# Page numbers bounded once on chip, and one register load for both parts of a value unit, in a decoder step on one core

## The chip, the cores and the metric

The kernel runs on one core of a Trainium2 chip. The metric is the device time of one execution in microseconds (us). The kernel before takes 4163.96 us, the median of 3 runs (4162.37 to 4166.68).

## The reference, cut to what matters

Two layers of a decoder are computed for a prompt (1024 tokens) and, with the same weights, for 8 sample sequences of 4 new tokens each. Everything is in float32. The change touches one part alone, how the samples read their past: 4096 old tokens for each of the 8, which lie in a pool of 320 pages of 128 tokens, at places that a table names.

```python
for l in range(DEPTH):                       # 2 layers
    xp, kp, vp, sp, cp, fp = trunk_layer(xp, lp, l, p_pos, ..., None, None, mk_p, mv_p, ...)   # the prompt
    past_k = cache_k[l][page_table].reshape(Bs, past_len, 2 * DIFF_H, DIFF_DH)   # page_table: 8 x 32 page numbers
    past_v = cache_v[l][page_table].reshape(Bs, past_len, DIFF_H, DIFF_DV)
    xs, ks_, vs_, ss, cs, fs = trunk_layer(xs, lp, l, s_pos, ..., past_k, past_v, ...)          # the samples

# trunk_layer, on h = rms_norm(x)
z = h @ w_in                                 # gated DeltaNet heads and differential attention heads side by side
x = x + concat([o_gdn, o_diff]) @ w_out
x = x + memory_attention(...) @ w_co         # cross-attention into 256 memory tokens
gt = causal_dwconv(hf @ w_gate)              # gated MLP, 2816 wide
x = x + (silu(gt) * (hf @ w_up)) @ w_down
```

## The kernel before, in words

**The prompt stream.** Per layer it projects (`w_in`), runs the DeltaNet heads and the causal attention, then the output projection, the cross-attention and the MLP. A float32 product is three matmuls of split operands. A weight unit is fetched into a `raw` tile by `fetch` (L359, a DMA issued by SyncE, here SP), ScalarE (ACT) copies it to `whi` (L376), GpSimd (POOL) makes `wlo` (L377), and TensorE (PE) multiplies. From the output projection on there are two `raw` slots, so a fetch may start when `wlo` of the unit before the last one is made. Just ahead of the output projection, `ot` tiles (two slots) bring the heads' outputs and eight DMAs bring back the residual (`x<-xsc`, L1826). In attention, `akT` and `aq` are the keys and queries, read back from DRAM (`qksc`).

**The sample stream.** `dec()` runs beside the prompt stream. A unit is 4 pages of one sequence, of keys or of values, 64 units of each kind in a layer. A unit is loaded in two halves, and each half fills one of four ring slots. A key half (`kn`) is 2 pages, whole: 2 DMAs of 256 KB. A value half (`vn`) is two quarters of each of the 4 pages: 4 DMAs of 128 KB, so the two value halves name the same 4 pages. Keys are transposed on VectorE (DVE, tile `T`) and multiplied into `psB`; values are multiplied into `psC`.

**How a page is addressed.** `pages` (L715) reads the page numbers from the row `pt_sb` in SBUF into SP's registers with one TENSOR_LOAD for each half, and with `min_val` and `max_val` given, each register is then checked: a FUSED_REGOPS computes whether it lies within the pool, and a SEQ_ASSERT reads that. After that each DMA has its own FUSED_REGOPS for its address, then a MOVE, then the issue itself (L724). All of this runs in order on SP, which also issues the weight fetches and most other DMAs.

**Order.** The program is written as generators that are interleaved by weights. Then a scheduler sets each engine's order with a timeline of its own, in which an instruction's cost plays a part. `issue_after` holds an instruction behind another: the page load stands behind the last page DMA and behind the last weight fetch written before it (`anchor`).

Of the kernel before, what the change touches and what calls it, by code (L numbers as in the profile page):

```python
# [9 lines left out]
F32 = mybir.dt.float32  # L10
# [4 lines left out]
ALU = mybir.AluOpType  # L15
# [8 lines left out]
NB = 8  # L24
# [6 lines left out]
NPG = PAST // P  # L31
# [154 lines left out]
def build(tc, a, out, depth=2):  # L186
    nc = tc.nc
# [38 lines left out]
    v_, s_, g_, t_ = Tracked(nc.vector), nc.scalar, nc.gpsimd, Tracked(nc.tensor)  # L226
# [273 lines left out]
    lp = lp_cm.__enter__()  # L500
# [30 lines left out]
    for t in range(9):  # L531
        n = P if t < 8 else NS
# [13 lines left out]
    for k0 in range(0, KT, 3):  # L546
# [3 lines left out]
        for k in range(m):  # L550
            if (k0 + k) % 2 == 0:
                t = dk.tile([P, 1056], F32R, name="pre", tag="pg", bufs=PGB).rearrange("p (a b c) -> p a b c", a=2, b=2)
# [8 lines left out]
        nc.sync.dma_start(xsc[:, :, csl(c)], x[:, :, csl(c)])  # L561
    pt_sb = cp.tile([1, NB * NPG], I32, name="pt_sb")
    nc.sync.dma_start(pt_sb, a["page_table"].rearrange("b n -> (b n)").unsqueeze(0))

    def scalars():
        for l in range(1, depth):
            params(l, nc.sync)
        for l in range(depth):
            lam_init = 0.8 - 0.6 * math.exp(-0.3 * l)
            lq = lp.tile([P, 4, 64], F32, name="lq", tag="lq", bufs=1)  # L570
            for k, nm in enumerate(("lam_q1", "lam_q2", "lam_k1", "lam_k2")):
                nc.sync.dma_start(lq[:, k, :], pbc(a[nm][l:l + 1, :]))
            pr = lp.tile([P, 2, 64], F32, name="pr", tag="pr")
            v_.tensor_tensor(pr, lq[:, 0:2], lq[:, 2:4], op=ALU.mult)
            sm = lp.tile([P, 2], F32, name="sm", tag="sm")
            v_.tensor_reduce(sm, pr, axis=AX.X, op=ALU.add)
            ex = lp.tile([P, 2], F32, name="ex", tag="ex")
            s_.activation(ex, sm, AF.Exp)
            nl = cp.tile([P, 1], F32, name=f"nlam{l}")
            v_.tensor_tensor(nl, ex[:, 1:2], ex[:, 0:1], op=ALU.subtract)  # L580
            v_.tensor_scalar(nl, nl, -lam_init, None, op0=ALU.add)
            lam_t.append(nl)
            ab = cp.tile([P, 2, 4], F32, name=f"ab{l}")
            nc.sync.dma_start(ab[:, 0, :], pbc(a["a_log"][l:l + 1, :]))
            nc.sync.dma_start(ab[:, 1, :], pbc(a["dt_bias"][l:l + 1, :]))
            abs_ = cp.tile([P, 2], F32, name=f"abs{l}")
            for h in range(4):
                v_.tensor_copy(abs_[32 * h:32 * h + 32, :], ab[32 * h:32 * h + 32, :, h])
            gate_b.append((ab, abs_))
# [76 lines left out]
    for l in range(depth):  # L666
# [23 lines left out]
        ckl, cvl = a["cache_k"][l], a["cache_v"][l]  # L690
        npool = ckl.shape[0]
# [13 lines left out]
        def ring(sh, nm, dt=F32):  # L705
            return dtile(sh, nm, "pg", PGB, 1056, dt)
# [6 lines left out]
                st_.enter_context(tc.issue_after(anchor[-1].ins))  # L713
                last_page.append(nc.sync.dma_start(dst, src))

        def pages(pg, n, dst, src):

            with ExitStack() as st_:
                if last_page:
                    st_.enter_context(tc.issue_after(last_page[-1].ins))  # L720
                st_.enter_context(tc.issue_after(anchor[-1].ins))
                _, regs = nc.values_load_multi_w_load_instructions(pt_sb[0:1, pg:pg + n], engines=(mybir.EngineType.SP,), min_val=0, max_val=npool - 1)
            for i, r in enumerate(regs):
                dma = nc.sync.dma_start(dst(i), src(r))  # L724
            last_page.append(dma)
# [7 lines left out]
        def dec():  # L733
# [15 lines left out]
            def load(i):  # L749
                if i >= 2 * len(seq):  # L750
                    return
                kind, b, S = seq[i // 2]
                hf = i % 2
                t = halves[i] = ring([P, 2, 512], kind + "n")
                if kind == "k":
                    pages(b * NPG + S * 4 + 2 * hf, 2, lambda j: t[:, j, :], lambda r: ckl[bass.ds(r, 1)].rearrange("o t h d -> (o t) (h d)"))
                else:
                    pages(b * NPG + S * 4, 4, lambda j: t[32 * j:32 * j + 32, :, :], lambda r: cvl[bass.ds(r, 1)].rearrange("o (i b) h e -> (o b) i (h e)", i=4)[:, 2 * hf:2 * hf + 2, :])

            cur = {}  # L760

# [41 lines left out]
            for i in range(PGB - 1):  # L803
                load(i)
            yield 0.1
            pT = po = None
            for i, (kind, b, S) in enumerate(seq):
                if kind == "k":
                    T = dtile([P, 4, 16, 32], "T", "T")
                    if b == 1 and S == 0:  # L810
                        queries(1)
                    for hf in range(2):
                        load(2 * i + hf + PGB - 1)
                        t = halves.pop(2 * i + hf)
                        with behind(v_):
                            v_.transpose(T[:, 2 * hf:2 * hf + 2].rearrange("p s j b -> p (s j b)"), t.rearrange("p s d -> p (s d)"))
                        yield 0.45
                    products(b, S, T)
                    yield 0.3
                    if b and S == 2:  # L820
                        pT = yield from transposed(b - 1)
                    continue
# [4 lines left out]
                if S == 1 and b + 2 < NB:  # L827
                    queries(b + 2)
                load(2 * i + PGB - 1)
                yield 0.5  # L830
                load(2 * i + PGB)
# [1530 lines left out]
        if more:  # L2362

            ws = []
            with prio(TPRI):
                for k0 in range(0, KT, 3):
# [3 lines left out]
                    for k in range(m):  # L2370
                        if (k0 + k) % 2 == 0:
                            t = ring([P, 2, 2, 264], "pre", F32R)
# [30 lines left out]
def program(inputs, depth=2):  # L2403
    import concourse.bacc as bacc

    nc = bacc.Bacc("TRN2", target_bir_lowering=False, num_devices=1)
    arrays, aps, outs = {}, {}, {}
    for name in _INS:
        arr = np.ascontiguousarray(inputs[name])
        arrays[f"in_{name}_dram"] = arr  # L2410
        aps[name] = nc.dram_tensor(f"in_{name}_dram", arr.shape, mybir.dt.from_np(arr.dtype), kind="ExternalInput").ap()
    arrays["in_cst_dram"] = CONST
    aps["cst"] = nc.dram_tensor("in_cst_dram", CONST.shape, F32, kind="ExternalInput").ap()
    for name, shape in _OUTS:
        outs[name] = nc.dram_tensor(f"out_{name}_dram", shape, F32, kind="ExternalOutput").ap()
    with tile.TileContext(nc, schedule_with_timeline_sim=True) as tc:
        build(tc, aps, outs, depth)
    return nc, arrays
# [8 lines left out]
```

## Time and profile before

| | |
|---|---|
| median of 3 runs | 4163.96 us |
| the profiled execution | 4172.92 us |
| its span, first to last instruction | 4171.1 us |
| TensorE busy | 3863.1 us (93%) |
| VectorE, ScalarE, GpSimd busy | 2256.6, 1311.7, 1174.7 us |
| mean granted TensorE clock | 0.957 of 2.4 GHz |
| page DMAs (keys, values) | 512 of 256 KB, 1024 of 128 KB |

SP has no line in the table of busy engines, because issuing a DMA and register work count as the sequencer's. Its instructions are found by their source line: L722 is the register load and its checks, L724 the page DMAs, L359 the weight fetches. "SPq" in a row is SP's sequencer. The profiled execution is 8.96 us longer than the median, so a sum over the trace is subtracted from 4172.92 and then set against the median.

### The profile page before, as it was taken

The numbers are of one execution on the slowest core, as the hardware profiler recorded it, in microseconds if no ns is written. First come the engines' busy times: TensorE is split into PE (matmuls) and PEld (weight loads), VectorE is DVE, ScalarE is ACT, GpSimd is POOL, SyncE is SP. The second block draws the span as 40 slices with busy tenths as digits, with TensorE's granted clock in tenths as the row PEclk, the third lists the DMA queues.
The fourth block names the chain that finished last, engine by engine and source line by source line (L and its number), as shares of the span: only waits on it lengthen the run. The fifth ranks groups of instructions, "written<-read, shape, count | busy, mean of one in ns | idle before, by whom it ended". The sixth has DMA issues, their size and how long they took to land. (4 is left out here: it accounts for less than half of the span.)

```text
span 4171.1 us, 72714 instructions
## 1 busy us (share of the span) xinstructions
PE 3863.1 (93%) x25178; PEld 2988.1 (72%) x25178; DVE 2256.6 (54%) x3907; ACT 1311.7 (31%) x2823; POOL 1174.7 (28%) x1125
## 2 busy tenths in 40 slices
PE   6899979979899999999979998889799999999999
PEld 5789866756667766776769987567566766677667
DVE  7355556863676544343367466577465734443334
ACT  4333424441442212321243253333334312222111
POOL 6452412222322212112246242132231311212211
PEclk8999979999999999999989999799899999999999
DMA  5464587647545543447427565764754455444751
GB/s 176 130 192 147 164 225 192 188 131 214 153 127 163 176 145 110 144 152 227 135 83 219 154 173 182 203 199 130 224 170 125 141 168 154 122 132 133 222 169 61
DMA packets 626469, 673.14 MB, mean 161 GB/s; under 512 B 76875, under 2 KB 444438, under 8 KB 626102
## 3 DMA queue, kind: packets, MB, share of 16 engines
q1 hardware_dynamic: 581475, 638.35, 51.4%
q10 hardware_dynamic: 42963, 25.81, 2.0%
q8 instruction: 200, 3.28, 0.3%
q0 software_dynamic: 1664, 4.33, 0.3%
q14 instruction: 167, 1.37, 0.1%
HBM read 588.12 MB, written 80.17 MB: 160 GB/s over the span
## 5 line engine op out<-in xcount | busy, mean ns | idle before, releaser
L377 POOL TENSOR_TENSOR wlo<-raw,whi 128x1024 fp32r<-128x1024 f32 (+1 forms) x308 | 531.0, 1736 | 1454.5 <-ACT whi L376 1349.5
L219 PE MATMUL psA<-hh,whi 128*128 128x512 f32 (+1 forms) x2096 | 794.1, 379 | 52.5 <-ACT whi L376 22.0
L219 PE MATMUL psA<-hl,whi 128*128 128x512 f32 (+1 forms) x2096 | 790.2, 377 | 4.4 <-DVE hl L219 2.7
L219 PE MATMUL psA<-hh,wlo 128*128 128x512 f32 (+1 forms) x2096 | 788.2, 376 | 0.0
L219 PEld LDWEIGHTS psA<-hh,whi 128*128 128x128 f32 x2096 | 399.7, 191 | 167.2 <-issue 34.0
L376 ACT CAST whi<-raw 128x1024 fp32r<-128x1024 f32 (+1 forms) x308 | 237.7, 781 | 766.0 <-PE psA L219 405.4
L219 PEld LDWEIGHTS psA<-hh,wlo 128*128 128x128 f32 x2096 | 399.2, 190 | 84.9 <-issue 27.2
L219 PEld LDWEIGHTS psA<-hl,whi 128*128 128x128 f32 x2096 | 400.9, 191 | 77.6 <-issue 14.9
L219 DVE STREAM_TRANSPOSE T<-kn 128x1024 f32<-128x1024 f32 x256 | 308.8, 1227 | 119.3 <-PE psB L219 109.6
L219 DVE TENSOR_TENSOR x<-x,psA 128x512 f32<-128x512 f32 x296 | 201.0, 683 | 248.0 <-PE psA L219 239.0
L219 DVE TENSOR_SCALAR fcv<-fraw,pvf 128x1024 f32<-128x1024 f32 x44 | 94.3, 2142 | 352.4 <-ACT fraw L2037 330.1
L219 PE MATMUL psG<-hh,whi 128*128 128x512 f32 x560 | 227.2, 406 | 0.9 <-ACT whi L376 0.9
L219 PE MATMUL psG<-hl,whi 128*128 128x512 f32 x560 | 225.6, 403 | 1.0 <-DVE hl L219 1.0
L219 PE MATMUL psG<-hh,wlo 128*128 128x512 f32 x560 | 223.8, 400 | 0.0
L219 PE MATMUL psA<-hi,hh 128*128 128x256 f32 (+1 forms) x720 | 205.4, 286 | 5.2 <-DVE cxn L219 4.1
L219 PE MATMUL psA<-ah,whi 128*128 128x512 f32 x484 | 195.7, 406 | 10.7 <-ACT whi L376 10.7
L219 PE MATMUL psA<-lo,hh 128*128 128x256 f32 (+1 forms) x720 | 203.8, 283 | 0.6 <-POOL lo L391 0.6
L219 PE MATMUL psA<-hi,hl 128*128 128x256 f32 (+1 forms) x720 | 204.4, 284 | 0.0
L219 PE MATMUL psA<-al,whi 128*128 128x512 f32 x484 | 195.0, 404 | 0.0
L219 PE MATMUL psA<-ah,wlo 128*128 128x512 f32 x484 | 193.9, 402 | 0.0
L219 PE MATMUL psA<-akT,aq 128*128 128x512 f32 (+7 forms) x384 | 154.5, 452 | 30.6 <-DMA aq<-qksc 30.6
L219 PE MATMUL psC<-vn,pT 128*32 128x512 f32 x1024 | 171.6, 626 | 7.8 <-DMA vn<-in_cache_v_dram 7.8
(516 smaller groups left out, 7331.0 us busy)
## 6 DMA issues: line engine op xcount, KB each, us to landing
kn<-in_cache_k_dram SPq DMA_DIRECT2D x512, 256.0 KB
vn<-in_cache_v_dram SPq DMA_DIRECT2D x1024, 128.0 KB
raw<-in_w_gate_dram SPq DMA_DIRECT2D x44, 512.0 KB
raw<-in_w_up_dram SPq DMA_DIRECT2D x44, 512.0 KB
raw<-in_w_down_dram SPq DMA_DIRECT2D x44, 512.0 KB
sw<-in_w_down_dram SPq DMA_DIRECT2D x44, 512.0 KB
sw<-in_w_gate_dram SPq DMA_DIRECT2D x48, 384.0 KB
sw<-in_w_up_dram SPq DMA_DIRECT2D x48, 384.0 KB
```

The lines of the kernel that those rows point to most:

```text
L219: r = f(*args, **kw)
L376: s_.copy(hi, raw)
L377: g_.tensor_tensor(lo, raw, hi.bitcast(F32), op=ALU.subtract)
```

## The change

Three instructions on VectorE now bound the row of page numbers once: to float, clamped to 0 and 319, back to integers. The numbers fit a float exactly, and the table's values lie within the pool, so nothing changes in them. With that, the check at each load is dropped (`skip_runtime_bounds_check_because`). And `pages` takes a key: the first half of a value unit keeps its 4 registers in `kept`, and the second half takes them from there instead of loading them again. Since only the load stood under `issue_after`, the second half's DMAs no longer stand behind the last weight fetch.

```diff
     pt_sb = cp.tile([1, NB * NPG], I32, name="pt_sb")
     nc.sync.dma_start(pt_sb, a["page_table"].rearrange("b n -> (b n)").unsqueeze(0))
+    ptf = lp.tile([1, NB * NPG], F32, name="ptf")
+    v_.tensor_copy(ptf, pt_sb)
+    v_.tensor_scalar(ptf, ptf, 0.0, float(a["cache_k"].shape[1] - 1), op0=ALU.max, op1=ALU.min)
+    v_.tensor_copy(pt_sb, ptf)
...
-        def pages(pg, n, dst, src):
+        kept = {}
+
+        def pages(pg, n, dst, src, keep=None):
 
             with ExitStack() as st_:
                 if last_page:
                     st_.enter_context(tc.issue_after(last_page[-1].ins))
                 st_.enter_context(tc.issue_after(anchor[-1].ins))
-                _, regs = nc.values_load_multi_w_load_instructions(pt_sb[0:1, pg:pg + n], engines=(mybir.EngineType.SP,), min_val=0, max_val=npool - 1)
+                regs = kept.pop(keep, None)
+                if regs is None:
+                    _, regs = nc.values_load_multi_w_load_instructions(pt_sb[0:1, pg:pg + n], engines=(mybir.EngineType.SP,), min_val=0, max_val=npool - 1, skip_runtime_bounds_check_because="the numbers were bounded on chip to those of the pool")
+                    if keep is not None:
+                        kept[keep] = regs
             for i, r in enumerate(regs):
                 dma = nc.sync.dma_start(dst(i), src(r))
             last_page.append(dma)
...
-                    pages(b * NPG + S * 4, 4, lambda j: t[32 * j:32 * j + 32, :, :], lambda r: cvl[bass.ds(r, 1)].rearrange("o (i b) h e -> (o b) i (h e)", i=4)[:, 2 * hf:2 * hf + 2, :])
+                    pages(b * NPG + S * 4, 4, lambda j: t[32 * j:32 * j + 32, :, :], lambda r: cvl[bass.ds(r, 1)].rearrange("o (i b) h e -> (o b) i (h e)", i=4)[:, 2 * hf:2 * hf + 2, :], (b, S))
```

The scheduler costs the shorter program anew, so the order moves. The next rows are SP's, before, in the MLP of layer 0, up to the eighth fetch of `w_down`. ISA is a register instruction, "ISA x8" are the four checks of a value half (a FUSED_REGOPS and a SEQ_ASSERT each), a single ISA is a DMA's address.

```order
L724 DMA vn_21739<-in_cache_v_dram 32x2x512
L722 TENSOR_LOAD pt_sb_425
L722 ISA x8
L724 ISA
L724 DMA vn_21810<-in_cache_v_dram 32x2x512
L724 ISA
L724 DMA vn_21810<-in_cache_v_dram 32x2x512
L724 ISA
L724 DMA vn_21810<-in_cache_v_dram 32x2x512
L724 ISA
L724 DMA vn_21810<-in_cache_v_dram 32x2x512
L359 DMA raw_21864<-in_w_down_dram 128x1024
```

The rows up to the same fetch now:

```order
L734 DMA vn_16041<-in_cache_v_dram 32x2x512
L734 ISA
L734 DMA vn_16041<-in_cache_v_dram 32x2x512
L734 ISA
L734 DMA vn_16084<-in_cache_v_dram 32x2x512
L734 ISA
L734 DMA vn_16084<-in_cache_v_dram 32x2x512
L734 ISA
L734 DMA vn_16084<-in_cache_v_dram 32x2x512
L734 ISA
L734 DMA vn_16084<-in_cache_v_dram 32x2x512
L359 DMA raw_16371<-in_w_down_dram 128x1024
```

The checks are gone, and between the two halves of a unit (`vn_16041`, `vn_16084`) no load stands any more. The fetch itself has moved: before it stood behind 456 value DMAs of the layer, now behind 416, so ten halves were ahead of it that now come after it. Of the 132 fetches of `w_gate`, `w_up` and `w_down` in the prompt stream, 26 moved against the page DMAs, 25 of them ahead and one behind. TensorE's order at this place is the same in both programs.

At the end of layer 0's projection SP's rows before are these, up to a fetch of `w_in` (the 80th of its kind):

```order
L722 TENSOR_LOAD pt_sb_425
L722 ISA x4
L724 ISA
L724 DMA kn_7521<-in_cache_k_dram 128x512
L724 ISA
L724 DMA kn_7521<-in_cache_k_dram 128x512
L722 TENSOR_LOAD pt_sb_425
L722 ISA x4
L359 DMA raw_7839<-in_w_in_dram 128x2x128
```

And now:

```order
L730 TENSOR_LOAD pt_sb_425
L734 ISA
L734 DMA kn_6228<-in_cache_k_dram 128x512
L734 ISA
L734 DMA kn_6228<-in_cache_k_dram 128x512
L997 DMA gdsc_80<-cdst_6312 128x1056
L1011 DMA out_p_gdn_conv_dram<-cso_6456 3x128
L1012 DMA out_s_gdn_conv_dram<-cso_6456 24x128
L359 DMA raw_6735<-in_w_in_dram 128x2x128
```

Eight key DMAs (four halves) that stood ahead of this fetch now come after it. On VectorE, in the prologue, the three new instructions stand among those of the first norms:

```order
L219 CAST ptf_427<-pt_sb_425 1x256
L219 TENSOR_TENSOR pr_792<-lq_787 128x128
L219 TENSOR_SCALAR ptf_427<-ptf_427 1x256
L219 TENSOR_REDUCE sm_794<-pr_792 128x2
L219 CAST pt_sb_425<-ptf_427 1x256
L219 TENSOR_TENSOR hl1_119<-nhf_224,hh1_117 128x2x352
```

## Rows read from the trace of the kernel before

**Rows 1.** The page: busy time, share of the span, instructions of each engine.
```profile
PE 3863.1 (93%) x25178; PEld 2988.1 (72%) x25178; DVE 2256.6 (54%) x3907; ACT 1311.7 (31%) x2823; POOL 1174.7 (28%) x1125
```
**Rows 2.** Waits of TensorE: who waited for whom, us in total, times, longest us.
```profile
PE psA L219 <- DVE cxn L219: 42.3, 7, 20.5
PE psA L219 <- ACT whi L376: 32.7, 9, 7.3
PE psA L219 <- DMA aq<-qksc: 30.6, 2, 17.1
...
PE psC L219 <- DMA vn<-in_cache_v_dram: 7.8, 5, 3.1
```
**Rows 3.** Instructions of L722, then L724: duration ns min/median/max, first and last start.
```profile
L722 SPq FUSED_REGOPS  x1536: 147/152/181, 179.4 to 3603.4; - x192
L722 SPq SEQ_ASSERT  x1536: 18/18/33, 179.6 to 3603.6; - x192
L722 SPq TENSOR_LOAD <-pt_sb x512: 293/468/1649, 178.5 to 3602.3; - x171
...
L724 SPq DMA_DIRECT2D vn<-in_cache_v_dram x1024: 316/317/1742, 412.3 to 3605.4; - x171
```
**Rows 4.** Timeline of SP, layer 0's MLP: start us, us, what.
```profile
1505.54 31.73 SPq L724 DMA_DIRECT2D vn<-in_cache_v_dram  x36
1537.38 0.37 SPq L359 DMA_DIRECT2D raw<-in_w_down_dram  x1
```
**Rows 5.** Timeline of GpSimd, then of TensorE, at the same place, [idle before <-releaser].
```profile
1506.91 2.42 POOL L377 TENSOR_TENSOR wlo<-raw,whi 128x1024 fp32r<-128x1024 f32 x1 [7.80 <-ACT whi L376]
...
1542.37 0.80 PE L219 MATMUL psA<-ah,whi 128*128 128x512 f32 x1 [4.96 <-ACT whi L376]
```
**Rows 6.** A stretch before: us, busy of PE, PEld, DVE, ACT, POOL, PEclk, DMA share, GB/s.
```profile
1400.00:1500.00 100.00, 100.00 (x660) 75.27 (x658) 54.91 (x57) 23.99 (x30) 23.63 (x15) 1.00 0.58 176
```
**Rows 7.** Timeline of TensorE at six other gaps.
```profile
551.66 0.66 PE L219 MATMUL psA<-hh,whi 128*128 128x352 f32 x1 [7.34 <-ACT whi L376]
...
2554.71 0.66 PE L219 MATMUL psA<-hh,whi 128*128 128x352 f32 x1 [6.36 <-ACT gt L339]
...
2620.21 1.59 PE L219 MATMUL psA<-akT,aq 128*128 128x128 f32 x5 [17.12 <-DMA aq<-qksc]
...
2967.85 1.65 PE L219 MATMUL psA<-hh,whi 128*128 128x512 f32 x3 [18.37 <-ACT hh L352]
...
3401.17 0.79 PE L219 MATMUL psA<-ah,whi 128*128 128x512 f32 x1 [5.70 <-ACT whi L376]
...
3534.90 0.50 PE L219 MATMUL psA<-hh,whi 128*128 128x512 f32 x1 [3.18 <-ACT whi L376]
```
**Rows 8.** Stretches, with the columns of rows 6.
```profile
1542.00:1549.00 7.00, 6.63 (x23) 4.38 (x24) 4.89 (x4) 1.36 (x2) 4.69 (x2) 0.66 0.31 82
3401.00:3408.00 7.00, 6.83 (x22) 4.61 (x22) 0.88 (x2) 1.16 (x2) 4.69 (x2) 0.57 0.37 106
3536.00:3541.00 5.00, 4.08 (x12) 3.18 (x12) 4.03 (x3) 0.96 (x1) 3.62 (x2) 0.66 0.54 150
...
2610.00:2640.00 30.00, 17.25 (x55) 10.02 (x55) 10.43 (x39) 8.11 (x29) 0.77 (x3) 0.50 0.98 220
```
**Rows 9.** Timeline of SP ahead of layer 1's output projection.
```profile
2953.78 2.56 SPq L1826 DMA_DIRECT2D x<-xsc  x5
...
2959.24 0.39 SPq L1823 DMA_DIRECT2D ot<-og  x1
```
**Rows 10.** Timeline of VectorE in the prologue.
```profile
47.84 0.43 DVE L219 CAST mlq<-mlqf 128x512 bf16<-128x512 f32 x1
```
**Rows 11.** Stretches, with the columns of rows 6: one part of each layer.
```profile
500.00:1000.00 500.00, 426.38 (x2951) 316.92 (x2950) 303.26 (x706) 177.10 (x537) 115.42 (x122) 0.91 0.68 192
2500.00:3000.00 500.00, 425.45 (x2998) 325.66 (x2997) 323.87 (x719) 183.99 (x547) 124.34 (x131) 0.88 0.64 188
```
**Rows 12.** Waits of SP itself.
```profile
SPq L359 <- POOL wlo L377: 452.7, 142, 21.4
```

## The prediction, on record before the changed kernel ran

> **What bounds the kernel now.** I began with the page's busy times: TensorE is busy 3863.1 of 4171.1 us [rows 1], which leaves 4171.1 − 3863.1 = 308 us without a matmul. No other engine comes near, so a change can pay only by closing such gaps, or by what the gaps do to TensorE's clock. The view of TensorE's waits says what ends them [rows 2]: a prologue wait for VectorE (20.5 us the longest), split weights (32.7 us), `aq` (30.6 us), value pages (7.8 us). The last three come, directly or through ScalarE, from DMAs that SP issues. So the next view was SP by source line [rows 3], and then its timeline just ahead of the gaps [rows 4].
>
> The MLP of layer 0 shows the pattern. From 1505.54 us on SP issues 36 value DMAs in 31.73 us, back to back, and only then, at 1537.38, the fetch of a `w_down` unit [rows 4]. Its `raw` slot had been free since GpSimd's `wlo` ended at 1506.91 + 2.42 = 1509.3 [rows 5]. TensorE, which ran without a pause a little earlier [rows 6], stands still for 4.96 us until ScalarE has split that unit [rows 5]. The fetch was 28 us late because SP's own work stood ahead of it, and a check for each of the 36 DMAs was part of that work.
>
> **What the change removes.** 1536 checks (256 key halves of 2 pages, 256 value halves of 4): a FUSED_REGOPS of 152 ns and a SEQ_ASSERT of 18 ns each [rows 3], 170 ns. And 512 − 384 = 128 register loads, at 293 to 468 ns [rows 3]. That is 1536 × 0.170 + 128 × 0.3 = 300 us of SP's time, or 320 with the upper figure. A value half loses 4 × 0.17 = 0.68 us, every second one 0.3 more. In the stretch above 36 DMAs are 9 halves of 3.5 us; they would come to some 2.7 us. None of it is on TensorE, so I go gap by gap.
>
> **The MLPs.** Three gaps end on a split weight: 4.96 [rows 5], 5.70 and 3.18 us [rows 7]. In the built order their fetches now stand ten value halves earlier (for the second, eight value and two key halves). Ten halves at 3.5 us are 35 us, more than the 28 us of lateness, so all three should close: 13.8 us. After each the granted clock is low for some us [rows 8]: 7.0 × (1 − 0.66) + 7.0 × (1 − 0.57) + 5.0 × (1 − 0.66) = 2.4 + 3.0 + 1.7 = 7.1 us of full clock lost. The granted level there is 1.2 instead of 2.4 GHz for a part of the stretch, each time after TensorE stood still. Together 20.9 us. Lower bound: nothing, if another weight of the same unit is late next.
>
> **Waits for value pages.** 7.8 us in 5 waits [rows 2]. SP issues value halves faster by a fifth to a quarter, and these waits are 1 to 3 us, so 0 to 7.8; I take 7.
>
> **The start of attention in layer 1.** TensorE waits 17.12 us for `aq` [rows 7]. Value halves stand ahead of those fetches on SP too, each shorter by 0.68 to 0.98 us now. But the DMA engines are 98% busy from 2610 to 2640 [rows 8]: an earlier issue there meets a full queue. The bounds are 0 and the gap, 17.1; I take 0, by that row. The Trainium skill says the same in "DMA: Bandwidth & Descriptors", section "Issuing engines are not separate DMA queues": all transfers run on the same 16 engines, and what is saved at the issuer is only its issue time, usually small beside the transfer. By that rule not only this term but the page waits too would come to nothing, 7 us less; the first term is where the rule does not fit, since there it was 28 us of issuing, not the transfer, that made the fetch late.
>
> **The end of layer 0's projection.** 7.34 us [rows 7], and the fetch now stands four key halves earlier. But the same place in layer 1 has a gap of 6.36 us that ScalarE's evacuation ends, not a weight [rows 7]. I take the difference, 1.0, with 0 and 7.3 as bounds.
>
> **The output projection of layer 1.** 18.37 us [rows 7]. `ot` is issued at 2959.24, behind the residual's DMAs [rows 9], and TensorE starts 8.6 us later; from a `w_down` fetch to its matmul it is 1542.37 − 1537.38 = 5.0 us [rows 4, 5]. In the built order the first `ot` tiles in question are issued ahead of those eight DMAs. I take 8.6 − 5.0 = 3.6, with 0 and 18.4 as bounds.
>
> **What is added.** Three instructions on VectorE, in the prologue, where TensorE waits 20.5 us on VectorE [rows 2]: this is on the path. The nearest row is a cast of 128x512 at 0.43 us [rows 10]; three of them are 1.3 us, the bounds 0 and 1.3, and I take 1.0. Their input's DMA is issued ahead of those of `lq`, which VectorE waits for anyway. Behind them on VectorE stand the norm's instructions, which TensorE waits for.
>
> **What is moved.** The scheduler reordered every engine a little. Such moves have both signs, and one pair of rows says what they are worth: 500 us of each layer at the same stage, ordered differently, hold 426.38 and 425.45 us of matmuls [rows 11]. Gaps that differ one by one add up to the same loss to 1 us. I read this as gaps of the stages with many short dependent steps (DeltaNet, attention) coming back elsewhere when one is closed, and count the three terms outside the MLPs, 7 + 1.0 + 3.6 = 11.6 us, at half: 5.8.
>
> **The sum.** 20.9 + 5.8 − 1.0 = 25.7 us from 4172.92 gives 4147.2; the median of the runs is 8.96 us below that execution, so 4138.
>
> **Rivals.**
>
> *No gain.* TensorE is the bound at 93%, SP's time is covered, and what an earlier fetch wins is lost at the next wait of ScalarE or VectorE. For it: the gaps named above are 13.8 + 7.8 + 17.1 + 7.3 + 18.4 = 64.4 of the 308 us, and rows 11 show that losses are tied to the stage rather than to one wait. Against it: ahead of the first MLP gap TensorE is busy 100.00 of 100 us [rows 6], so there nothing waits to take its place. Time: 4164, give or take 8. The Trainium skill's "Perfetto Trace Analysis", section "Identifying the Most-Contended Engine", would have it so: the engine with the highest occupancy is to be optimized first, and this change touches one that is not it. The same page's next section says to look for the gaps and what blocks them, which is what I follow.
>
> *Slower: a fetch that waits in front.* 25 weight fetches now stand ahead of page DMAs that they stood behind. If the `raw` slot is not free yet, SP stops at the fetch and all pages behind it stop too; the sample stream's matmuls stand at fixed places in TensorE's order, so TensorE then waits for pages. SP's waits for a slot are 452.7 us in 142 now, 3.2 us each [rows 12]. For it: a fetch moved ahead by 35 us where the slot has been free for 28 gets in front of its slot by some us. Against: four ring slots of pages lie between SP and TensorE. It decides once more than 25.7 / 3.2 = 8 of the 25 waits reach TensorE in full; with half of them, 12.5 × 3.2 = 40 us, the time is 4138 + 40 = 4178.
>
> *Much faster.* Every term at its upper end: 20.9 + 7.8 + 17.1 + 7.3 + 18.4 = 71.5, less the 1.0 of the prologue: 70 us, 4094. It begins at a gain of 45. For it: SP is freed of 300 us, and no view shows all that stood behind it. Against: rows 11.
>
> **How the numbers follow.** The forecast (a gain of 10 to 45 us) has 0.55, much faster 0.15, no gain 0.17, slower 0.13. What a measurement of this kernel can tell from no change is 0.2%, 8.3 us. All of the first two cases is faster, 0.70; of no gain nearly all is the same, 0.17; slower is 0.13. The forecast's own range is 4119 to 4154. To hold 8 in 10 I take most of the faster case and the no-gain case up to its end: 4100 to 4170.
>
> **What would show it.** L722's rows gone and register loads 384; in the MLPs the three gaps closed and their clock rows at 1.00; SP's timeline with waits for `psC` or `wlo` where it now runs without one; the value waits below 3 us in sum. The forecast is wrong in its main step if the MLP gaps stand as they are, or come back at another unit with the fetch early; wrong in the halving if the whole 11.6 us or more comes outside the MLPs; and the slower rival is right if TensorE's waits for `vn` grow while SP's waits for `wlo` do.

## The result, and the profile after

The changed kernel takes **4087.13 us**, the median of 4 runs (4080.95 to 4096.89); beside them the kernel before took 4163.16 us (4 runs, 4161.38 to 4166.68). The ratio is **0.9823, 95% interval 0.9808 to 0.9837**: 76 us or 1.8% faster. The forecast was 4138 us with a range of 4100 to 4170: the sign was right, the size was not, and the time lies below the range. The rival "much faster" (4094 us) was the one that came.

The profiled execution after has a span of 4079.2 us against 4171.1. That is 92 us, more than the 76 of the medians: the traced execution of before lay 9 us above its median, that of after 6 below. So sums over the two traces are compared with 92.

TensorE's line of the page, then the waits of TensorE (who waited for whom, us in total, times, longest), as in [rows 1, 2]:

```profile
PE 3828.3 (94%) x25178; PEld 2968.2 (73%) x25178; DVE 2259.1 (55%) x3909; ACT 1309.5 (32%) x2822; POOL 1182.1 (29%) x1125
```
```profile
PE psA L219 <- DVE cxn L219: 41.6, 5, 20.4
PE psA L219 <- ACT whi L376: 24.2, 7, 9.5
...
PE psA L219 <- DMA aq<-qksc: 13.3, 2, 7.9
PE psC L219 <- DMA vn<-in_cache_v_dram: 10.3, 6, 4.5
...
PE psB L219 <- DVE T L219: 9.5, 3, 8.2
```

Two things are to be seen. TensorE is busy 34.8 us less with the same 25178 matmuls, so more than a third of the 92 us is not a wait at all but matmuls that pass faster. And the waits for pages did not shrink: those for values are 10.3 us, where [rows 2] had 7.8.

SP's instructions of the register load (L730) and the page transfers (L734), duration ns min/median/max, which answer to [rows 3]:

```profile
L730 SPq TENSOR_LOAD <-pt_sb x384: 295/472/1310, 198.6 to 3501.8; - x192
```
```profile
L734 SPq FUSED_REGOPS  x1536: 37/46/56, 199.5 to 3508.0; - x192
...
L734 SPq DMA_DIRECT2D vn<-in_cache_v_dram x1024: 316/317/1562, 410.0 to 3508.2; - x171
```

The checks are gone; the 1536 register operations that are left make the addresses, as before. All of SP's instructions together cover 1866 us in the trace of before and 1561 in this one: 305 us less, as the forecast had it (300 to 320).

The place in layer 0's MLP that the forecast started from, on SP (start us, us, what; answers to [rows 4]):

```profile
1485.56 0.37 SPq L359 DMA_DIRECT2D raw<-in_w_down_dram  x1
1488.08 11.39 SPq L734 DMA_DIRECT2D vn<-in_cache_v_dram  x16
1499.57 0.40 SPq L359 DMA_DIRECT2D raw<-in_w_gate_dram  x1
1501.71 10.74 SPq L734 DMA_DIRECT2D vn<-in_cache_v_dram  x16
```

The same `w_down` unit, the eighth of the layer, is fetched at 1485.56 instead of 1537.38, ahead of the value transfers instead of behind 36 of them. TensorE no longer stands still there.

Where the 92 us are, is seen by the stretch. The tables below give the time between the same two matmuls in each trace, named by their time in the trace before. First the rows of before, then those of after, each for the MLP of layer 0, the DeltaNet and attention stretch of layer 1, the MLP of layer 1, and the stretch of layer 0 (columns as in [rows 6]):

```profile
1350.00:1700.00 350.00, 344.42 (x1827) 245.21 (x1826) 157.58 (x194) 76.39 (x98) 69.82 (x47) 0.99 0.51 153
2500.00:3000.00 500.00, 425.45 (x2998) 325.66 (x2997) 323.87 (x719) 183.99 (x547) 124.34 (x131) 0.88 0.64 188
3350.00:3700.00 350.00, 340.20 (x1754) 239.53 (x1753) 146.63 (x194) 73.73 (x93) 65.29 (x46) 0.99 0.49 148
450.00:1000.00 550.00, 476.38 (x3269) 361.47 (x3269) 329.23 (x752) 203.90 (x585) 143.66 (x161) 0.92 0.67 189
```
```profile
1338.00:1675.00 337.00, 337.00 (x1829) 243.41 (x1828) 159.02 (x194) 76.48 (x98) 70.32 (x47) 1.00 0.54 157
2469.00:2933.00 464.00, 412.61 (x3002) 313.95 (x3001) 311.93 (x713) 184.77 (x551) 119.49 (x128) 0.94 0.71 202
3281.00:3609.00 328.00, 328.00 (x1753) 236.09 (x1750) 153.82 (x196) 75.22 (x96) 67.56 (x46) 1.00 0.53 157
448.00:995.00 547.00, 476.31 (x3269) 358.32 (x3268) 337.90 (x756) 202.40 (x580) 146.61 (x157) 0.92 0.68 189
```

The two MLPs give 13.3 + 21.8 = 35.1 us (to a tenth, by the matmuls' starts), and TensorE is now busy in them all the time at a granted clock of 1.00. Layer 1's DeltaNet and attention stretch gives 36.5 us, layer 0's only 2.8. The rest of the 92 us, 18, lies in pieces of up to 7 us over the other stretches.

| stretch (matmuls by their time in before) | before | after | difference |
|---|---|---|---|
| 450 to 1000, DeltaNet and attention, layer 0 | 549.9 | 547.1 | −2.8 |
| 1350 to 1700, MLP, layer 0 | 350.1 | 336.8 | −13.3 |
| 2500 to 3000, DeltaNet and attention, layer 1 | 500.0 | 463.5 | −36.5 |
| 3350 to 3700, MLP, layer 1 | 350.0 | 328.2 | −21.8 |

### The profile page after: what moved, and what is told of

The parts are those of the page before. It is cut to its first block, busy times and chain, and to the rows that moved or that the text cites. A ratio compares the mean times of both kernels' runs of the same rounds, so it can differ in the third digit from the quotient of the medians.

```text
span 4079.2 us, 69558 instructions
## 1 busy us (share of the span) xinstructions
PE 3828.3 (94%) x25178; PEld 2968.2 (73%) x25178; DVE 2259.1 (55%) x3909; ACT 1309.5 (32%) x2822; POOL 1182.1 (29%) x1125
## 5 line engine op out<-in xcount | busy, mean ns | idle before, releaser
L219 DVE TENSOR_SCALAR fcv<-fraw,pvf 128x1024 f32<-128x1024 f32 x44 | 107.3, 2439 | 315.3 <-ACT fraw L2047 294.9
L219 PE MATMUL psA<-akT,aq 128*128 128x512 f32 (+7 forms) x384 | 155.1, 451 | 13.9 <-DMA aq<-qksc 13.3
L219 PE MATMUL psC<-vn,pT 128*32 128x512 f32 x1024 | 157.3, 618 | 10.3 <-DMA vn<-in_cache_v_dram 10.3
```

Of the source, the lines that this page charges most:

```text
L219: r = f(*args, **kw)
```

## The experiments

The change does two things at once. It takes 260 to 265 us of checks (by the traces) and some 40 us of loads out of SP's stream, and, since the scheduler that sets the order counts SP's work, it gives another order. Two theories follow: **issue time** (what counts is SP's time itself) and **order** (what counts is where the instructions now stand). Every ratio is to the kernel before, on the same chip, with its 95% interval.

### Order and checks, crossed

The scheduler's order is a list of instructions for each engine, so it can be kept while the checks are taken out of it, or put in. Here the order of before, without checks:

```diff
+def drop_checks(nc):   # after scheduling: three register operations and an assertion, 1536 times
+    ...
+    blk.instructions = [i for i in blk.instructions if i.name not in out]
     ...
         build(tc, aps, outs, depth)
+    drop_checks(nc)
```

> The order of every engine is that of the kernel before; only the 1536 checks (three register operations and an assertion each, some 172 ns by the rows of before: 152 to 154 ns and 18 ns) are taken out of SyncE's stream. Theory 'issue time': the 264 us of SyncE that they cost are what the fetches waited for, so this kernel gets most of the 76 us in proportion to SyncE's time (264 of 307 us): about 4098 us, ratio 0.984. Theory 'order': the gain came from where weight fetches stand among page transfers; then this stays near before, at most the 5 to 15 us of the value pages: 4150 to 4160 us, ratio 0.996 to 0.999.

And the order of after, with 1536 checks put back:

```diff
                 dma = nc.sync.dma_start(dst(i), src(r))
+                if i == 0:
+                    CHECKED.append((dma.ins.name, regs))
     ...
+    put_checks(nc)     # after scheduling: a check of each register ahead of the unit's first transfer
```

> The order of every engine is that of the kernel after, register loads shared and bounding kept; but 1536 checks stand in SyncE's stream again, ahead of each unit's first page transfer. Theory 'issue time': the 264 us are back and with them most of the time: about 4153 us, ratio 0.998. Theory 'order': it stays near after, 4087 to 4100 us, ratio 0.982 to 0.985.

| ratio | order of before | order of after |
|---|---|---|
| with 1536 checks | 1 | 0.9932 (0.9916 to 0.9947) |
| without | 0.9904 (0.9888 to 0.9920) | 0.9823 (0.9808 to 0.9837) |

Neither theory stands alone. The checks cost 40 us in the order of before and 45 in that of after; the order (with the shared registers) is worth 28 us with checks and 34 without. The sum of the two alone is 68 of 74 to 76 us: they nearly add up. But they act in different places. In the MLPs the new order gives 33.6 us with all checks in SP's stream, while taking the checks out of the old order gives 13.5. The first four rows are the order of after with checks, the last four the order of before without; each has the MLP of layer 0, the DeltaNet and attention stretch of layer 1, the MLP of layer 1 and the stretch of layer 0 (columns as in [rows 6]):

```profile
1370.00:1706.00 336.00, 336.00 (x1825) 242.60 (x1824) 158.76 (x194) 75.70 (x97) 70.26 (x47) 1.00 0.53 159
2504.00:2989.00 485.00, 419.10 (x3001) 317.23 (x3000) 312.80 (x713) 184.87 (x551) 119.42 (x128) 0.92 0.67 193
3335.00:3665.00 330.00, 329.65 (x1755) 236.64 (x1752) 154.18 (x196) 75.19 (x96) 67.54 (x46) 1.00 0.53 158
450.00:1025.00 575.00, 488.63 (x3267) 369.88 (x3268) 338.41 (x758) 202.00 (x580) 146.16 (x160) 0.89 0.64 179
```
```profile
1330.00:1674.00 344.00, 342.94 (x1829) 243.76 (x1828) 157.77 (x194) 76.66 (x99) 69.91 (x47) 1.00 0.51 155
2470.00:2957.00 487.00, 420.50 (x2994) 320.18 (x2994) 322.24 (x719) 184.14 (x547) 123.93 (x131) 0.90 0.66 192
3306.00:3649.00 343.00, 338.74 (x1752) 238.30 (x1751) 144.11 (x194) 73.73 (x93) 65.69 (x46) 0.99 0.49 149
448.00:988.00 540.00, 468.89 (x3270) 354.87 (x3269) 334.01 (x753) 203.59 (x584) 142.86 (x161) 0.93 0.69 192
```

In the DeltaNet and attention stretches it is the other way round. With the checks put back, the order of after needs 575.2 us in layer 0 and 484.4 in layer 1, where it needs 547.1 and 463.5 without them: 28 and 21 us. In the order of before the same checks cost 10 and 12.

### One part of the change at a time

Bounding and no checks, but every half loads its own registers:

```diff
-    ...rearrange("o (i b) h e -> (o b) i (h e)", i=4)[:, 2 * hf:2 * hf + 2, :], (b, S))
+    ...rearrange("o (i b) h e -> (o b) i (h e)", i=4)[:, 2 * hf:2 * hf + 2, :])
```

> Numbers bounded on chip and checks left out, but each part of a value unit loads its own registers (512 loads), scheduled anew. Theory 'issue time': 264 of the 307 us of SyncE are gone: about 4098 us, ratio 0.984. Theory 'value units' (what counted is that a value unit's second part no longer stops for a load): little, 4140 us or more. Theory 'order': not tied to either sum; anything from 4080 to 4165 us.

Registers shared, no bounding, checks at the 384 loads:

```diff
-    ..., max_val=npool - 1, skip_runtime_bounds_check_because="...")
+    ..., max_val=npool - 1)
```

> Registers shared by both parts of a value unit, checks kept at the 384 loads that are left (1024 checks), no bounding. By SyncE's time 128 loads of some 0.34 us and 512 checks of 0.172 us go, 131 us of 307. Theory 'issue time': 131/307 of 76 us: about 4131 us, ratio 0.992. Theory 'value units': most of the gain, 4095 to 4110 us. Theory 'order': not tied to the sum.

They came out alike, 0.9882 (0.9866 to 0.9897) and 0.9882 (0.9865 to 0.9899). "Issue time" in proportion would set them 33 us apart and is refuted as a rule; "value units" had 4140 us for the first and 4095 to 4110 for the second, and got 4112 and 4113. Either part alone gives the scheduler's order in the MLPs (336.8 us in layer 0 for both). What the two give only together lies in layer 1's DeltaNet and attention stretch: 488.2 and 488.1 us alone, 463.5 together.

The bounding alone:

```diff
+    v_.tensor_copy(ptf, pt_sb)
+    v_.tensor_scalar(ptf, ptf, 0.0, float(a["cache_k"].shape[1] - 1), op0=ALU.max, op1=ALU.min)
+    v_.tensor_copy(pt_sb, ptf)
```

> Only the bounding is added: three instructions of VectorE in the prologue, checks and loads as before, no transfer moved on SyncE. Forecast term: 1.0 us, between 0 and 1.3: ratio 1.000 within 0.001.

0.9988 (0.9977 to 1.0000). The three instructions cost nothing that can be seen. This kernel fetches in the very order of before, and its stretches tell the scatter of one trace: 351.3 and 349.9 us in the MLPs, but 493.6 instead of 500.0 in layer 1's DeltaNet and attention stretch. So of the 36.5 us there, some 30 can be relied on.

### The change parted by place

The checks are left out only for the page units loaded from the output projection on (`i >= 120`), with no sharing. On SP this moves 26 of the MLPs' 336 weight transfers among the pages, 25 of them ahead. The expectation says that no other weight moves; in the trace 8 fetches of the cross-attention's weights just before the MLPs (`w_cq`, `w_co`) have moved ahead too:

```diff
+    skip_runtime_bounds_check_because="..." if unchecked else None    # unchecked: i >= 120
```

> Numbers bounded on chip; the checks are left out only for the 136 page units of each layer that are loaded from the output projection on (those beside the cross attention and the MLP), 864 of 1536; registers not shared. In SyncE's order only the weight fetches of the MLPs move (26 of 336). Theory 'parts add up': the two MLPs give what they gave in the kernel after, 13 and 22 us, the rest nothing: 4163 - 35 = 4128 us, ratio 0.9915. Theory 'comes back elsewhere' (the halving of the prediction, taken to the MLPs too): half of it, 4146 us, 0.996.

The complement (`i < 120`):

> The complement: checks left out only for the first 120 page units of each layer (beside projection, DeltaNet and attention), 672 of 1536; in SyncE's order one MLP fetch moves, and the others move as with all checks off. Theory 'parts add up': what all checks off gave (0.9882, 49 us) less the 35 us of the MLPs: 14 us, 4149 us, 0.9966. Theory 'comes back elsewhere': nothing, 4163 us, 1.000.

And the first of the two with its 864 checks put back after scheduling, so that only the place of these 34 fetches, and the order on TensorE that came with it, is left of the change:

> The order of the kernel with checks off from the output projection on, and the 864 checks put back into SyncE's stream ahead of each unit's first transfer: only the place of 26 weight fetches, and what follows from it on TensorE, is left of the change. Theory 'order': the MLPs keep 33 of 35 us: 4130 us, 0.992. Theory 'issue time': they lose it, 4155 to 4163 us, 0.998 to 1.000.

| | ratio | MLP of layer 0 | MLP of layer 1 |
|---|---|---|---|
| before | 1 | 350.1 | 350.0 |
| checks off beside the MLPs | 0.9889 (0.9875 to 0.9903) | 336.8 | 328.2 |
| the same order, checks put back | 0.9926 (0.9913 to 0.9938) | 338.7 | 333.9 |
| checks off beside DeltaNet and attention | 0.9987 (0.9976 to 0.9999) | 347.3 | 350.3 |

For the MLPs this parts the two theories. The place of these fetches, with TensorE's order that came with it, is worth 31.5 us of 4162, and 27.5 of them lie in the MLPs (the expectation had 33 of 35 kept there); with the checks out it is 45, of which 35 lie in the MLPs. Checks off beside DeltaNet and attention are worth 6 us by themselves. The two parts add up: 45 + 6 = 51, and all checks off gave 49. So here the MLPs' gain does not come back elsewhere. One pair of runs limits this: all checks off in a new order (0.9882) is only 9 us faster than checks off in the order of before (0.9904), though its MLPs are 22 us shorter; outside the MLPs that new order is the worse one. The theory of "issue time" had 0 to 7 us for the kernel with checks put back, "order" 32: the latter holds. SP there, with the 864 checks put back, at layer 0's `w_down`:

```profile
1494.83 5.37 SPq L734 DMA_DIRECT2D vn<-in_cache_v_dram  x8
1500.30 0.37 SPq L359 DMA_DIRECT2D raw<-in_w_down_dram  x1
1502.31 12.63 SPq L734 DMA_DIRECT2D vn<-in_cache_v_dram  x16
```

16 value transfers take 12.63 us here and 11.39 without checks, yet the fetch is early and its wait is gone.

### Loads, and orders made with checks that are not run

Registers kept for key units too (256 loads), almost in the order of after:

```diff
+    pages(b * NPG + S * 4, 4, ..., ("k", b, S), (2 * hf, 2 * hf + 2))     # 4 numbers loaded, 2 used by each half
```

> The kernel after, and in it one register load of four page numbers for both parts of a key unit too: 256 loads instead of 384; the order is after's but for 108 of SyncE's 3013 transfers. Theory 'issue time': 128 loads of 0.46 us go, 59 us of SyncE's time, which at the rate of the checks (45 us of the span for 265 us of SyncE's time in after's order) is 10 us: 4077 us, ratio 0.980. Rival 'dead time': the loads stand where SyncE waits for buffers anyway, no change, 0.982. Rival 'order': the moved transfers decide, 4065 to 4105 us.

0.9811 (0.9796 to 0.9827), against 0.9823 (0.9808 to 0.9837) for after: 128 loads less bring nothing that these intervals tell apart. The medians are 4086.90 and 4087.13. In the traces the loads' time fell by more than the expectation's 59 us, from 176 to 84 us, since the median of those left is 0.30 us instead of 0.47. The expected 10 us are not excluded by the intervals, and the order moved a little, so "dead time" is the nearer theory but not shown.

The next three take an order that was made with checks and then drop the checks, as above, with the numbers bounded on chip: all of the order from the kernel with shared registers and checks; all of it with key units shared as well; only layer 0's (`if l else None` at the skip, so that layer 1 is scheduled without).

> The order that is made with shared registers and 1024 checks (that of the run with sharing alone, 0.9882); then these checks are taken out of SyncE's stream, and the numbers are bounded on chip. Theory 'issue time': 1024 checks of 0.173 us, 177 us of SyncE's time, at the same rate 30 us: 4083 us, ratio 0.981. Rival 'the MLPs are done': the two MLPs have their whole gain already in this order, so only the 12 to 20 us of the DeltaNet and attention stretches come: 4093 to 4100 us, ratio 0.983 to 0.985.

> Registers of key and value units shared, order made with the checks of the 256 loads that are left, then the checks taken out; numbers bounded on chip. Theory 'issue time': SyncE's stream is that of the keys-shared kernel, so its time is too, 4077 us, ratio 0.980, whatever the order. Theory 'order': it differs from that kernel by 10 us or more, to either side, since 342 of SyncE's transfers stand elsewhere than with sharing alone.

> The order of layer 0 is made with checks (as with sharing alone), that of layer 1 without; then the checks of layer 0 are taken out of SyncE's stream. Theory 'order': layer 0's DeltaNet and attention stretch (450 to 1000 us) gets the order of sharing alone, 543.9 us there with checks, some 535 without, against 547.1 in after; the rest as in after: 4075 us, ratio 0.979. Rival: layer 1's order shifts too and loses its 24 us against the other orders: 4095 to 4100 us, ratio 0.985.

| | ratio | 450 to 1000 | 2500 to 3000 |
|---|---|---|---|
| shared registers with checks | 0.9882 (0.9865 to 0.9899) | 543.9 | 488.1 |
| that order, checks dropped | 0.9851 (0.9838 to 0.9865) | 532.8 | 484.3 |
| key units shared too, checks dropped | 0.9831 (0.9817 to 0.9844) | 538.0 | 479.6 |
| only layer 0 so | **0.9790 (0.9777 to 0.9803)** | 532.2 | 463.0 |
| after | 0.9823 (0.9808 to 0.9837) | 547.1 | 463.5 |

In the order with shared registers 1024 checks were worth 13 us by the ratios, where "issue time" had 30; the MLPs had their gain already, as the rival said, though 4102 lies a little above its 4093 to 4100. The same SP work in another order differs by 20 us in layer 1. Layer 0's better order and layer 1's better order go together: that kernel, at 4074.33 us, beats before and after; its expectation was 4075. The order with key units shared too stays undecided: 0.9831 against 0.9811 for the same SP work in the order made without checks, with intervals that overlap, where "order" had asked for 10 us or more and "issue time" for none.

### The two parts of a value unit on TensorE

The matmuls of the MLPs got 19.7 us shorter (busy 344.5 to 336.8 and 340.2 to 328.2), and low clock explains only a part. Here are the value products in TensorE's timeline, first of before, then of after (start us, us, what). A product is two matmuls in the trace, so x4 is one half of a unit and x8 a whole one:

```profile
1580.51 1.05 PE L219 MATMUL psC<-vn,pT 128*32 128x512 f32 x4
1581.50 0.50 PE L219 MATMUL psA<-hh,whi 128*128 128x512 f32 x1
```
```profile
1553.58 1.06 PE L219 MATMUL psC<-vn,pT 128*32 128x512 f32 x8
1554.58 0.50 PE L219 MATMUL psG<-hh,whi 128*128 128x512 f32 x1
```

A half by itself holds TensorE for 1581.50 − 1580.51 = 0.99 us, a whole unit for 1554.58 − 1553.58 = 1.00. The products of a unit write four separate strips of 32 rows of `psC` and run at the same time; two run as long as four. Two halves apart cost 0.98 us more than a unit, 0.49 for each half. In the MLPs of before 10 and 17 halves stand alone, in those of after 0 and 4. This is TensorE's order, which the new program changes too. The section on the change has it as the same at the eighth `w_down` fetch, but that holds for the weights' products alone: of the 96 matmuls of `w_down` there, value units stand behind the 31st and (two) the 87th in before, and behind the 6th, the 74th and the 78th in after. The Trainium skill's "TensorEngine Tiling (Array Packing)", section "When to Use Tiling", has a left operand with a free dimension of 32 as the case for four tiles side by side; the rows agree, and they add that two of four save nothing.

Four kernels tested it. In three the products of the second half are issued first and the first half's behind them, so that a unit stays whole:

```diff
-                    for j in range(4):
-                        t_.matmul(po[32 * j:32 * j + 32, :], ...)
+                    for j in (2, 3, 0, 1):
+                        with ExitStack() as st_:
+                            if lead is not None:
+                                st_.enter_context(tc.issue_after(lead.ins))
+                            m = t_.matmul(po[32 * j:32 * j + 32, :], ...)
+                        lead = lead or m
```

> The kernel before, all checks and loads kept; only TensorE's order of a value unit's four products is held together (the two of the second part first, the two of the first right behind), so that 2 parts instead of 56 stand alone. Theory 'parts apart': a part alone takes TensorE 0.97 us, a whole unit 0.96 us, so 27 units save 26 us: 4136 us, ratio 0.994, and most of it in the MLPs (13 of the 27). Rival 'buffers': the first part holds its buffer until the second has come, pages are fetched later, and it is no faster or slower than before: 4160 us or more.

> The kernel after with the same hold: 2 parts instead of 26 stand alone. Theory 'parts apart': 12 units of 0.97 us, 12 us: 4075 us, ratio 0.979. Rival 'buffers' or 'order': 4087 us or more, 0.982 or above.

> The fastest kernel so far (layer 0's order made with checks that are then taken out, ratio 0.979) with the same hold. Theory 'parts apart': 13 units, 13 us: 4062 us, ratio 0.976. Rival 'order': layer 0's or layer 1's good order is lost with it, 4075 to 4095 us.

In the fourth the two halves' products stand apart in the code, with a `yield 0.25` between them:

> The kernel after with the two parts of a value unit put apart in the code (a step of the other work between them): 103 parts alone instead of 26. Theory 'parts apart': 38 units more at 0.97 us, 37 us slower: 4124 us, ratio 0.991. Rival: a part alone runs beside the other work at no cost: 4087 us, 0.982.

The price of a half alone is confirmed where nothing else moves: in the MLPs, TensorE busy without a pause. The first two rows are the MLPs with 16 and 18 halves alone (after: 0 and 4, 337 and 328 us), the last is layer 1's MLP of after with 0 instead of 4:

```profile
1349.00:1695.00 346.00, 346.00 (x1827) 243.55 (x1827) 156.81 (x194) 76.21 (x98) 70.26 (x47) 1.00 0.52 153
3332.00:3669.00 337.00, 337.00 (x1755) 236.90 (x1755) 152.65 (x195) 75.15 (x96) 66.08 (x44) 1.00 0.52 152
```
```profile
3298.00:3624.00 326.00, 325.77 (x1750) 236.07 (x1750) 153.22 (x195) 75.19 (x96) 66.93 (x45) 1.00 0.55 158
```

9.3 us for 16 halves, 8.9 for 14, −1.9 for −4: 0.5 to 0.6 us each. As a remedy it fails: 0.9986 (0.9976 to 0.9996) for before, 0.9838 (0.9824 to 0.9851) for after, and 0.9834 (0.9820 to 0.9847) for the fastest, which gets slower by it; put apart, 0.9934 (0.9920 to 0.9947), by the ratios some 46 us above after. In before the MLPs' matmuls get 14.3 us shorter, but 6.2 us come back as waits for weights, and layer 0's DeltaNet and attention stretch gets 8.5 us longer. In after, layer 1's stretch loses its good order (484.1 us). Both rivals, "buffers" and "order", were nearer than the sum of halves. Putting them apart cost more than the 37 us of the halves, but there layer 1's stretch lost its good order too (488.7 us, 25 more than in after), and the MLPs gave 18 of the 46 us.

## Why the prediction was right or wrong

**SP's time and where it stood in the way: right.** 305 us of SP's instructions went, and the late `w_down` fetch was the mechanism in the MLPs. Most of the 305 us reappears as waits of SP for free buffers. The first two rows are of before, beside [rows 12], the next three of after:

```profile
SPq L724 <- DVE T L219: 265.6, 80, 13.9
SPq L724 <- PE psC L219: 73.5, 33, 9.1
```
```profile
SPq L359 <- POOL wlo L377: 538.2, 161, 22.4
SPq L734 <- DVE T L219: 304.8, 87, 12.2
SPq L734 <- PE psC L219: 208.5, 77, 13.7
```

These three waits grew by 86, 39 and 135 us, 260 in sum.

**The MLPs, 20.9 us: the mechanism right, the size too small.** They gave 35.1. TensorE's idle time in them was 15.4 us (13.8 counted, in three gaps) and all of it went. The clock was a term of 7.1 us. What the sum left out is the 23 halves of value units that stood alone, 23 × 0.49 = 11.3 us. 35.1 − 15.4 − 11.3 leaves 8.4 us for the clock and for what is small. The missing term is seen by itself in the order of before without checks: its layer 0 MLP has only 1.1 us idle and a clock of 1.00, and is still 6.8 us longer than after's; 10 halves alone are 4.9 of that. The forecast counted waits, and this cost stands in TensorE's busy time.

**Value pages, 7 us: wrong.** TensorE's waits for values went from 7.8 to 10.3 us, and those for the keys' transposes (`T`) to 9.5 from the row below, which is of before. The row behind it, of the order of after with the checks put back, has the values at twice that.

```profile
PE psB L219 <- DVE T L219: 3.9, 3, 1.4
```
```profile
PE psC L219 <- DMA vn<-in_cache_v_dram: 19.9, 12, 4.8
```

SP's time alone did what the term said: in the order of before without checks the value waits are 1.9 us. The new order makes pages later, mostly in layer 0's DeltaNet and attention stretch, and the checks' time pays for part of it. It is not the 25 fetches of the slower rival: with those moved and every check in place the value waits are 9.4 us, only 2.1 of them in an MLP. The sign that the forecast named for that rival did appear, the waits for `vn` (7.8 to 10.3) and those for `wlo` (452.7 to 538.2) both grew, and the kernel was faster all the same. The sign had no size; in the MLPs of after TensorE waits for no page.

**The start of attention in layer 1, 0 us: the step failed.** The forecast let the gap stand because the DMA engines are 98% busy [rows 8]. It is 17.12 us before, 13.91 in the same order without checks, and in after it is two waits, 7.12 and 5.38 (first that row, with the sum of that kernel's waits for `aq`, then those of after):

```profile
2582.14 1.60 PE L219 MATMUL psA<-akT,aq 128*128 128x128 f32 x5 [13.91 <-DMA aq<-qksc]
...
PE psA L219 <- DMA aq<-qksc: 30.8, 2, 16.9
```
```profile
2568.32 0.37 PE L219 MATMUL psG<-c_ident,tk 128*2 128x128 f32 x1 [7.12 <-POOL tk L1168]
...
2576.10 1.60 PE L219 MATMUL psA<-akT,aq 128*128 128x128 f32 x5 [5.38 <-DMA aq<-qksc]
```

With the evacuation just ahead of it (`gt`, 6.36 us [rows 7]) this place went from 23.5 to 12.5 us. From the issue of the first `aq` to the matmul it is 7.2 us in before, 7.6 without checks and 8.2 in after, so the transfers themselves did not get faster: the gap is shorter because the issue comes earlier against TensorE, which in after also has other products to do in between. How much of that is SP's time is not shown. In the order of before the 3.2 us won in layer 1 are lost in layer 0, where the same wait grows from 13.5 to 16.9 us; the waits for `aq` are 30.8 us in sum without checks and 30.6 with them [rows 2], and 13.3 in after. The rule of the Trainium skill that the prediction weighed here, in "DMA: Bandwidth & Descriptors", section "Issuing engines are not separate DMA queues", has the issue time that is saved as usually small beside the transfer. For `aq` the runs do not decide it. For the whole kernel what is saved at SP was not small: its checks alone, with no transfer changed and none moved, were worth 40 us.

**The output projection of layer 1, 3.6 us: too small.** The gap was 18.37 us and ended on `ot`; it is 9.47 and ends on a weight:

```profile
2898.16 0.80 PE L219 MATMUL psA<-hh,whi 128*128 128x512 f32 x1 [9.47 <-ACT whi L376]
```
```profile
2919.00 1.65 PE L219 MATMUL psA<-hh,whi 128*128 128x512 f32 x3 [20.40 <-ACT hh L352]
```

The second row is the kernel after with joined products: there, as in every other kernel here that has no checks in SP's stream and needs 479 us or more in this stretch, TensorE waits 15 to 23 us for `ot`. In the order of after with the checks put back that wait is gone too, so the order ends it.

**The halving, 11.6 to 5.8 us: the step that failed most.** The paragraph "What is moved" took a reordering as a loss that comes back elsewhere in the same stage. It was read from two stretches of before that hold the same 426 us of matmuls in 500 us [rows 11]. In after, those two stretches differ: layer 1's shrank by 36.5 us, layer 0's by 2.8. With the 18 us of the other stretches that is 57 us outside the MLPs, where the forecast had 11.6 even before it halved them. The equal sums were a coincidence, and the two windows did not hold the same work: layer 1 comes to its output projection 468 us into its window (2967.85, [rows 7]), layer 0 439 us into its own:

```profile
939.33 0.80 PE L219 MATMUL psA<-hh,whi 128*128 128x512 f32 x1 [6.66 <-ACT whi L376]
```

What came instead is seen where order and checks are crossed (one trace each, with some 6 us of scatter). In these two stretches the checks alone are worth 22 us in the order of before (10 and 12) and 49 in that of after (28 and 21): what SP's time gives there does not come back. The order alone shortens layer 1's by 16 us with checks and 24 without, and lengthens layer 0's by 25 and 7. So the moves did have both signs, but they do not cancel in a layer, and the forecast had no term for that. Without checks in SP's stream the orders here need 463 to 489 us in layer 1's stretch and 532 to 551 in layer 0's; that after has the best in layer 1 and one of the worst in layer 0 was luck as far as the forecast goes. Of layer 1's 36.5 us, 12.8 are busy time (425.45 and 412.61 in the rows of the two stretches) at a granted clock of 0.88 before and 0.94 after; the forecast counted the clock in the MLPs alone. Checks off beside these stretches alone gave 6 us, near the halved sum, but in yet another order.

**The added VectorE work, −1.0 us:** not seen; the prologue's wait stayed at 20.4 us.

**"Much faster"** was right in size, for other reasons: not every gap closed, and more than a third of the gain was matmul time.

What stays open: why the scheduler finds layer 1's good order only with both parts of the change, or with checks kept in layer 0's schedule. That the order makes it is shown; which of its moves does is not.

## What to carry to other kernels

Work on a queue that is nobody's bottleneck counts twice: as time ahead of what stands behind it, and as a cost by which a scheduler sets the order; keep the order and drop the work, then drop the order and keep the work, and the two come apart. A stretch's busy time is to be compared too, not only its waits: products that run side by side when they stand together cost double when the order parts them. When a scheduler draws anew for every edit, an order that is good in one stretch can be kept there and another taken elsewhere.

## What the runs showed of the hardware that was not expected

- Two products on 64 of the 128 rows of `psC` take as long as four on all: 1.05 us for x4, 1.06 for x8.
- 260 to 265 us of register checks on SP, with no transfer moved, cost 40 to 45 us of a kernel whose TensorE is busy 93% of the time.
- 128 register loads fewer, 92 us of SP's time in the traces, changed nothing that can be told (ratio 0.9811 against 0.9823, intervals that overlap), in an order that is almost the same.
